# Sixty 128-wide turns moved from TensorE to VectorE's 32x32 blocks, with short-piece transfers that place the blocks

## The chip, the cores and the metric

The kernel runs on one core of one Trainium2 chip. The metric is device time in microseconds (us) of one execution, as a median of runs; lower is better. On the core, TensorE (PE) does matrix products and turns (transposes through an identity matrix) into PSUM banks, VectorE (DVE) and ScalarE (ACT) do element-wise work and empty the banks, GpSimd (POOL) does small work, and SyncE (SP) issues nearly all transfers (DMAs) in one queue, in order.

## What is computed

One layer of an encoder for two groups of tokens: 512 prompt tokens and 64 sample tokens that have caches. All in float32.

```
xn   = rmsnorm(x, ln_mix);  proj = xn @ w_in        # conv input, z, gates, q/k/v of differential attention
h    = x + [gated delta net ; differential attention] @ w_out
mk   = rmsnorm(mem, ln_mem_kv) @ w_mem_k            # prompt: from 256 memory rows; also an output
mv   = rmsnorm(mem, ln_mem_kv) @ w_mem_v            # also an output
h    = h + softmax(q mk^T) mv @ w_mem_o             # sample: mk, mv come from cache_mem_k, cache_mem_v
h    = h + relu(rmsnorm(h) @ w_ff1)^2 @ w_ff2
y    = rmsnorm(h, ln_final)
```

The keys of the differential attention of the sample are `cache_diff_k` (256 rows) and 64 new rows; the new keys of both groups are outputs too (`o_dk_p`, `o_dk_s`). `rmsnorm(x, g)` is x times g times one over the root of the mean square of the row.

## The kernel before

**Layout.** Activations lie turned: feature on the 128 partitions, token along the row. `project` multiplies weight blocks of 128 columns with them. Each float32 weight is split in a high part `wh` (ACT cast, L573) and a remainder `wl` (DVE, L574), and products are done in three terms. A weight block of 512 KB is loaded by SP at L564 or L569 into one of four `raw` buffers.

**Order.** The program is traced in one order and then rearranged: `Arrangement` (L161 to L328) plays it through with a model of each engine's times (`Step.cost`, L119), picks at each step what can start first, and fixes the order of every engine's queue by `arrange` (L419). For a DMA it takes 530 ns of SP's time (L405), a rate by row length (L138) and 2500 ns to spare on the landing (L407). The order of PE's queue is thus fixed when the program is built. Of SP's transfers that are ready, the one traced first goes first.

**Where data must be turned.** Four places have rows where columns are needed, or the reverse, and use `tr` (L532), a PE instruction on a 128x128 block that writes a PSUM bank with tag `ba`:

- *Memory rows*: `mt` (L1040) holds the 256 memory rows of 1024, loaded in one DMA (L1041). `turn_memory` (L1350) takes the squares (ACT, L622), the root (DVE and POOL), multiplies root and gain row `gkv` in (L1352, helper L632), turns 16 blocks (L1354) and splits them into `mh` and `ml` (L1356, L1357). These are the fixed operands of the two memory projections from L1619; these put their banks in `dst` at L1639.
- *Key output*: in `diff_project` (L1406) the key projection of each of four heads arrives turned in `kdT`. `evac` turns 2 blocks per half of the prompt and 1 of the sample (L1461, L1463), copies them to `ko` (L1471, L1474) and stores them (L1472, L1475). `ko` shares the two buffers `p0` with `ckr[0]` and with the softmax tiles of `diff_head` (L1507). Behind it SP places the stacked copies of keys and queries (L1437, L1456, L1458) that the scores read.
- *Cached keys*: `diff_cache` (L1481) loads 256 rows in 2 DMAs (L1485), turns 8 blocks (L1488) and copies them to `ckT` (L1489). The sample's scores read it (L1496).
- *Cached memory keys*: `cm` (L1709) is loaded in one DMA (L1710) into storage slot 5 once the product with `w_out` has read that slot; 16 blocks are turned (L1722) and split into `cmT` and `cml` (`split_turned`, L1596). Slot 5 next takes the first memory attention output `mo` (L1770), written at L1784 and L1785.

Of the kernel before, what the change touches and what calls it, by code (L numbers as in the profile page):

```python
# [9 lines left out]
F32 = mybir.dt.float32  # L10
# [421 lines left out]
def hybrid_layer_kernel(  # L432
# [76 lines left out]
    def small(tag, shape, bufs=None, dt=F32):  # L509
        tag = SHARED.get(tag, tag)  # L510
        bufs = 1 if tag in ("vn", "on", "S", "qz", "an", "B0") or tag[:-1] in ("At", "Dt", "Y") else 2
        return sp.tile(shape, dt, tag=tag, name=nm(tag), bufs=bufs)
# [19 lines left out]
    def tr(out, in_):  # L532
        n = in_.shape[0]
        nc.tensor.transpose(out, in_, ident[:n, :n])  # L534
# [10 lines left out]
    def gain_rows(g, tag):  # L545
        gB = cp.tile([P, D], F32, tag=tag, name=nm("gB"))
        nc.sync.dma_start(gB, g.partition_broadcast(P))
        return gB
# [71 lines left out]
    def squares(dst, src, n):  # L620
        s1 = tiny([P, 1])
        A.activation(dst[:n], src[:n], AF.Square, accum_out=s1[:n])  # L622
        return s1

    def root(s1, n, total=None):
        r1 = tiny([P, 1])
        V.tensor_scalar(s1[:n], s1[:n] if total is None else total, 1.0 / D, EPS, ALU.mult, ALU.add)
        rpow(r1[:n], s1[:n])
        return r1

    def scale(dst, src, r1, gB, n, c=slice(0, D)):
        V.scalar_tensor_tensor(dst[:n, c], src[:n, c], r1[:n], gB[:n, c], ALU.mult, ALU.mult)  # L632
# [234 lines left out]
    with after(last_traced()):  # L867
        G.memset(triu, 1.0)
        G.affine_select(out=triu, in_=triu, pattern=[[1, P]], compare_op=ALU.is_ge, fill=0.0, base=0, channel_multiplier=-1)
    G_Q, G_FF, G_FIN = 16, 24, 32  # L870
    gn = gcol[:, 40:41]
    dn = const([P, 1], "dn")
    V.tensor_scalar(dn, gcol[:, 41:42], 1.0 - LAM0, None, ALU.mult)
# [165 lines left out]

    mt = view(e3, 0, 2, D)  # L1040
    nc.sync.dma_start(mt, mem_prompt[0].rearrange("(b p) d -> p b d", p=P))  # L1041
    gkv = gain_rows(ln_mem_kv[0], "qz1")
    mn = view(e5, 0, 2, D)
    mhl = pair(4, F32R)
    mh, ml = view(mhl, 0, KT, NMEM), view(mhl, 1, KT, NMEM)
# [26 lines left out]
    def v4(ap, nb):  # L1072
        return ap.rearrange("p (h n) -> p h n", h=4)[:, :nb, :]

    def sb(tag, bufs=2):
        return small(tag, [P, 4, P], bufs)

    zs, zsample = (
        ap.rearrange("p (h t) -> p h t", h=H)
# [269 lines left out]

    def turn_memory():  # L1350
        for bi in range(2):
            scale(mn[:, bi, :], mt[:, bi, :], root(squares(mn[:, bi, :], mt[:, bi, :], P), P), gkv, P)  # L1352
            for q in range(2):
                src = turn(mn[:, bi, :], P, q, "ba")  # L1354
                mhi, mlo = (x[:, 4 * q : 4 * q + 4, bi * P : (bi + 1) * P] for x in (mh, ml))
                A.copy(mhi, src)  # L1356
                V.tensor_tensor(mlo, src, mhi.bitcast(F32), ALU.subtract)  # L1357

    S, behind = None, lambda: None
    prepared = [gdn_prep(*chunks[0])]  # L1360
# [39 lines left out]
    with after(*behind_keys):  # L1400
        G.memset(qz[64:, :64], 0.0)
        G.memset(qz[:64, 64:], 0.0)
        G.memset(vs[64:], 0.0)
    stacked = {}

    def diff_project(h):  # L1406
        hs = slice(h * P, (h + 1) * P)
        if h < 2:
            qn = [od[:, 2 * h + j, :SEQ].bitcast(F32R) for j in range(2)]
        else:  # L1410
            qn = [small(tag, [P, SEQ], dt=F32R) for tag in ("Y0", "Y1")]
        tags = ("kd", "vb", "X", "KQ") if h % 2 else ("At0", "At1", "Dt0", "Dt1")
        ks = [small(tag, [P, SEQ], dt=F32R) for tag in tags]
        stacked[h] = ks[:2], ks[2:]
        for kind, base in (("q", 2056), ("k", 2568), ("v", 3080)):
            def evac(b, a0, n):
                first_half = a0 == 0
                t0 = slice(0, 256) if first_half else slice(256, SEQ)

                def parts(dst, src):  # L1420
                    A.copy(dst[0][:, t0], src)
                    V.tensor_tensor(dst[1][:, t0], src, dst[0][:, t0].bitcast(F32), ALU.subtract)

                if kind == "q":
                    d = qn[1][:, t0].bitcast(F32)
                    with tc.high_priority():
                        scaled(d, b[:, :256], a0)
                        parts(qn, d)
                    if first_half:
                        for c in range(2):  # L1430
                            R = slice(64 * c, 64 * c + 64)
                            V.tensor_tensor(qz[R, R], b[R, 256:], rB[R, 256:320], ALU.mult)
                    else:
                        for c in range(2):
                            R = slice(64 * c, 64 * c + 64)
                            for j in range(2):
                                nc.sync.dma_start(  # L1437
                                    qs[h % 2][64 * j : 64 * j + 64, c, :SEQ].bitcast(F32), qn[j][R].bitcast(F32)
                                )
                    return  # L1440
                if kind == "v":
                    d = small("zr", [P, 320])
                    dp_, ds = d[:, :256], d[:, 256:]
                else:
                    dp_, ds = kdT[:, h, t0], kdT[:, h, SEQ:T]
                with tc.high_priority():
                    scaled(dp_, b[:, :256], a0)
                    if first_half:
                        scaled(ds, b[:, 256:], 256)
                if kind == "k":  # L1450
                    parts(stacked[h][0], dp_)
                    if not first_half:
                        first_, second_ = ([x.bitcast(F32) for x in pair_] for pair_ in stacked[h])
                        for j in range(2):
                            for R in (slice(0, 64), slice(64, P)):
                                nc.sync.dma_start(second_[j][R], first_[j][64:])  # L1456
                        for j in range(2):
                            nc.sync.dma_start(first_[j][64:], first_[j][:64])  # L1458
                bt = bank()
                for t in range(2):  # L1460
                    tr(bt[:, t * P : (t + 1) * P], dp_[:, t * P : (t + 1) * P])  # L1461
                if first_half:
                    tr(bt[:DEC, 256:384], ds)  # L1463
                src, t2 = bt[:, :256].rearrange("p (t d) -> p t d", t=2), slice(t0.start // P, t0.start // P + 2)
                if kind == "v":
                    A.copy(vtm[:, t2, hs], src)
                    if first_half:
                        A.copy(vs[:DEC, h, :], bt[:DEC, 256:384])
                else:
                    ko = small("ko", [P, 3, P])  # L1470
                    A.copy(ko[:, :2], src)  # L1471
                    nc.sync.dma_start(o_dk_p[0, 0, t0, h, :].rearrange("(t p) d -> p t d", p=P), ko[:, :2])  # L1472
                    if first_half:
                        A.copy(ko[:DEC, 2], bt[:DEC, 256:384])  # L1474
                        nc.sync.dma_start(o_dk_s[0, 0, :, h, :], ko[:DEC, 2])  # L1475

            project(weights(w2, base + h * P), xs, evac, halves=GATHERED)
        nc.sync.dma_start(o_dv_p[0, 0, :, h, :].rearrange("(t p) d -> p t d", p=P), vtm[:, :, hs])
        nc.sync.dma_start(o_dv_s[0, 0, :, h, :], vs[:DEC, h, :])

    def diff_cache():  # L1481
        ckr = [small("p0", [P, 512]), small("p1", [P, 512])]
        nc.sync.dma_start(cvv, cache_diff_v[0, 0].rearrange("(b p) h d -> p b (h d)", p=P))
        for bi in range(2):
            nc.sync.dma_start(ckr[bi], cache_diff_k[0, 0, bi * P : (bi + 1) * P].rearrange("p h d -> p (h d)"))  # L1485
            b = bank()
            for h in range(H):
                tr(b[:, h * P : (h + 1) * P], ckr[bi][:, h * P : (h + 1) * P])  # L1488
            A.copy(ckT[:, :, bi * P : (bi + 1) * P], v4(b, 4))  # L1489

    def sample_rows(h, hs, so, on):

# [126 lines left out]
    for w, out in ((w_mem_k, o_mk), (w_mem_v, o_mv)):  # L1619
        dst = tokens  # L1620
        for f in range(2):
# [14 lines left out]
                                start=(k == 0 and j == 0), stop=(k == KT - 1 and j == 2),  # L1636
                            )
            for t in range(2):
                (A.copy if t else V.tensor_copy)(dst[:, t, fs], bs[t])  # L1639
                if out is o_mv:  # L1640
                    A.copy(mv[:, t, fs], dst[:, t, fs])
                    V.tensor_tensor(mvl[2 * t + f], dst[:, t, fs], mv[:, t, fs].bitcast(F32), ALU.subtract)
# [63 lines left out]
    V.tensor_scalar(shrink16, cols, -1.0 / 16, None, ALU.mult)  # L1706


    cm = view(pair(5), 0, 2, D)  # L1709
    nc.sync.dma_start(cm, cache_mem_k[0, 0].rearrange("(b p) h d -> p b (h d)", p=P))  # L1710
    cmu = pair(2, F32R)
    cmv = [small(tag, [P, 512]) for tag in ("X", "X", "B0", "B0")]
    for j, cv_ in enumerate(cmv):
# [2 lines left out]
    cmT, cml = (view(cmu, i, KT, NMEM) for i in range(2))  # L1716
    mkl, cml = ([x.rearrange("p (j n) -> p j n", j=2) for x in mkl], [cml[:, 2 * i : 2 * i + 2, :] for i in range(4)])
    for k2 in range(KT // 2):
        b = bank()
        for kk in range(2):  # L1720
            for bi in range(2):
                tr(b[:, kk * 256 + bi * P : kk * 256 + (bi + 1) * P], cm[:, bi, (2 * k2 + kk) * P : (2 * k2 + kk + 1) * P])  # L1722
        split_turned(cmT[:, 2 * k2 : 2 * k2 + 2, :], cml[k2], b)

    mo = []
    for h in range(H):
# [557 lines left out]
```

## Time and profile before

| | |
|---|---|
| median of 3 runs | 919.6 us (919.39 to 919.87) |
| the profiled execution, its own time | 918.87 us |
| its span | 917.1 us |
| PE busy | 907.4 us |
| DVE busy | 763.0 us |
| ACT busy | 622.3 us |
| turns of the four places, on PE | 16 + 20 + 8 + 16 = 60 |

The span runs from the first to the last instruction of the profile; 1.8 us of the execution lie around it. "Busy" of PE is a union of instruction spans whose ends are modelled, so a few tenths of a us between starts can be waits. Turns carry the line of the helper, L534, and name the bank (`ba`, `g`) and the tile (`u` for the large tiles, `p` for `p0` and `p1`). A merged row of the timeline gives the start of its first instruction, the time to the end of its last, and the count.

### The profile page before, as it was taken

How to read it: one execution, taken by the hardware profiler on the slowest of the kernel's cores; microseconds unless marked ns; L12 is line 12 of the kernel's file. 1: busy time of each engine (PE TensorE's matmuls, PEld its weight loads, DVE VectorE, ACT ScalarE, POOL GpSimd, SP SyncE). 2: the span in 40 equal slices, each digit the busy share in tenths (PEclk: the TensorE clock that was granted, in tenths of full speed). 3: DMA queues.
4: the chain of work that ended last, by engine and by line, in shares of the span. 5: the costliest groups of instructions: out<-in, count | busy, mean ns of one | idle time of the engine just before them, and what ended most of it. 6: DMA issues, size and time to landing. Idle time of an engine off the chain costs nothing.

```text
span 917.1 us, 17313 instructions
## 1 busy us (share of the span) xinstructions
PE 907.4 (99%) x6482; PEld 873.6 (95%) x6482; DVE 763.0 (83%) x1658; ACT 622.3 (68%) x1418; POOL 71.6 (8%) x165
## 2 busy tenths in 40 slices
PE   8999999999999999999999999999999999999997
PEld 7999999999999888999999999999999999999986
DVE  6878887988787776666557989999999999999995
ACT  6564885535566664435445658878888888888855
POOL 2452112110010000000000000000000000000001
PEclk9999999999999999999999999999999999999999
DMA  6923411116444857341211322332323223322313
GB/s 200 300 64 92 117 54 36 36 47 175 119 120 113 280 191 206 86 129 56 59 46 51 112 68 76 99 94 87 108 92 94 92 93 93 92 93 93 115 48 104
DMA packets 112287, 96.97 MB, mean 106 GB/s; under 512 B 6888, under 2 KB 99274, under 8 KB 111690
## 3 DMA queue, kind: packets, MB, share of 16 engines
q1 hardware_dynamic: 111450, 94.67, 34.7%
q8 instruction: 51, 0.84, 0.4%
q10 hardware_dynamic: 656, 1.18, 0.4%
q14 instruction: 34, 0.28, 0.1%
q0 software_dynamic: 96, 0.00, 0.0%
HBM read 80.85 MB, written 9.75 MB: 99 GB/s over the span
## 4 chain that ended last, share of the span: by engine, by line
PE 95%; ACT 3%; DVE 1%; DMA 1%; issue 0%; SPq 0%; ACTq 0%
PE pr L530 57%; PE g L530 13%; PE ba L530 12%; PE gs L530 7%; PE ba L534 3%; PE g L534 2%; ACT w L1806 1%; DMA raw<-in_w_in_dram 1%; DVE w L1807 0%; ACT wl L1806 0%; ACT pr L2064 0%; PE gs L534 0%; PE ba L2156 0%; PE pr L2156 0%; ACT wh L1806 0%; DVE raw L1902 0%
## 5 line engine op out<-in xcount | busy, mean ns | idle before, releaser
L530 PE MATMUL pr<-u,wh 128*128 128x320 f32 (+3 forms) x1608 | 364.9, 317 | 1.6 <-ACT wh L726 0.9
L530 PEld LDWEIGHTS pr<-u,wh 128*128 128x128 f32 x1608 | 262.1, 189 | 10.9 <-ACT u L793 1.1
L530 PE MATMUL pr<-u,wl 128*128 128x320 f32 (+2 forms) x984 | 256.9, 299 | 0.0
L530 PEld LDWEIGHTS pr<-u,wl 128*128 128x128 f32 x984 | 174.2, 189 | 1.0
L573 ACT CAST wh<-raw 128x1024 fp32r<-128x1024 f32 x65 | 68.3, 1050 | 62.8 <-PE pr L530 52.2
L574 DVE TENSOR_TENSOR wl<-raw,wh 128x1024 fp32r<-128x1024 f32 x65 | 79.4, 1222 | 26.7 <-ACT wh L573 26.1
L1807 DVE TENSOR_TENSOR w<-raw,w 128x512 fp32r<-128x512 f32 x89 | 60.1, 688 | 6.5 <-PE pr L530 2.3
L1806 ACT CAST w<-raw 128x512 fp32r<-128x512 f32 x89 | 52.9, 619 | 3.2 <-DVE raw L1902 2.3
L530 PE MATMUL ba<-u,wl 128*128 128x288 f32 x360 | 52.6, 295 | 0.0
L2067 ACT COPY u<-pr 128x288 f32<-128x288 f32 x116 | 46.1, 398 | 5.6 <-PE pr L530 3.9
L530 PEld LDWEIGHTS ba<-u,wl 128*128 128x128 f32 x360 | 49.3, 188 | 0.0
L530 PE MATMUL pr<-x,w 128*128 128x288 f32 x252 | 46.9, 294 | 0.0
L530 PE MATMUL pr<-u,w 128*128 128x288 f32 x252 | 46.9, 294 | 0.0
L530 PE MATMUL pr<-wh,u 128*128 128x512 f32 x128 | 41.8, 399 | 0.0
L2064 ACT COPY pr<-u 128x288 f32<-128x288 f32 x100 | 39.5, 403 | 2.7 <-DVE u L2069 1.0
L2069 DVE TENSOR_TENSOR u<-u,pr 128x288 f32<-128x288 f32 x80 | 35.9, 450 | 6.2 <-PE pr L530 5.9
L1807 DVE TENSOR_TENSOR wl<-raw,wl 128x512 fp32r<-128x512 f32 x58 | 39.0, 684 | 0.2
L530 PEld LDWEIGHTS pr<-x,w 128*128 128x128 f32 x252 | 38.0, 187 | 0.0
L530 PEld LDWEIGHTS pr<-u,w 128*128 128x128 f32 x252 | 38.0, 188 | 0.0
L1806 ACT CAST wl<-raw 128x512 fp32r<-128x512 f32 x58 | 34.3, 621 | 4.2 <-PE ba L530 2.1
L530 PE MATMUL pr<-x,wl 128*128 128x288 f32 x168 | 31.9, 297 | 0.2
L530 PE MATMUL pr<-x,wh 128*128 128x288 f32 x168 | 31.6, 296 | 0.1
(564 smaller groups left out, 2050.8 us busy)
## 6 DMA issues: line engine op xcount, KB each, us to landing
raw<-in_w_ff_dram SPq DMA_DIRECT2D x36, 512.0 KB
raw<-in_w_ff_dram SPq DMA_DIRECT2D x56, 256.0 KB
raw<-in_w_in_dram SPq DMA_DIRECT2D x27, 512.0 KB
raw<-in_w_mem_k_dram SPq DMA_DIRECT2D x8, 512.0 KB
raw<-in_w_mem_v_dram SPq DMA_DIRECT2D x8, 512.0 KB
raw<-in_w_out_dram SPq DMA_DIRECT2D x8, 512.0 KB
raw<-in_w_mem_q_dram SPq DMA_DIRECT2D x8, 512.0 KB
raw<-in_w_mem_o_dram SPq DMA_DIRECT2D x8, 512.0 KB
```

Source lines behind the costliest of these rows:

```text
L530: nc.tensor.matmul(out, lhsT, rhs, start=start, stop=stop, skip_group_check=skip_group_check)
L534: nc.tensor.transpose(out, in_, ident[:n, :n])
L573: A.copy(wh, raw)
L574: V.tensor_tensor(wl, raw, wh.bitcast(F32), ALU.subtract)
L1806: A.copy(hi, src)
L1807: V.tensor_tensor(lo, src, hi.bitcast(F32), ALU.subtract)
L2064: A.copy(b[:, :n], to)
L2067: A.copy(to, b[:, :n])
L2069: V.tensor_tensor(to, to, b[:, :n], ALU.add)
```

## The change

All four places take another way. A 32x32 block is turned inside VectorE (`V.transpose`, one instruction over a whole row of blocks), and a DMA puts the blocks where they belong, for each group of 32 columns one DMA whose contiguous pieces are 32 floats (128 bytes).

- `turned_in`: four DMAs load 256 rows by 128 columns so that the 32x32 blocks lie in the place of their turned position; one `V.transpose` of 128x256 then finishes the turn. Used for the memory rows (8 times, 32 DMAs), the cached keys (4 times, 16 DMAs) and the cached memory keys (8 times, 32 DMAs).
- `turned_out`: `V.transpose` first, then four DMAs store. Used for the key output: per head 8 DMAs for the prompt and 4 for the sample, 48 in all.
- The memory rows are turned unscaled. The gain is multiplied in when they are split (`gcol`, a scalar for each partition), and the root of the norm (`mroot`, a scalar for each row) when the banks of the memory projections are evacuated. The load of the gain rows `gkv` and the two products of L1352 go; the load of `mt` and the squares stay, and the squares write to `mn`, where the new blocks are loaded.

```diff
+    def turned_in(dst, src):
+        for a in range(0, P, 32):
+            rows_ = src[:, a : a + 32].rearrange("(b p) c -> p b c", p=32)
+            nc.sync.dma_start(dst[a : a + 32].rearrange("p (b c) -> p b c", c=32), rows_)
...
-            scale(mn[:, bi, :], mt[:, bi, :], root(squares(mn[:, bi, :], mt[:, bi, :], P), P), gkv, P)
-            for q in range(2):
-                src = turn(mn[:, bi, :], P, q, "ba")
-                mhi, mlo = (x[:, 4 * q : 4 * q + 4, bi * P : (bi + 1) * P] for x in (mh, ml))
-                A.copy(mhi, src)
-                V.tensor_tensor(mlo, src, mhi.bitcast(F32), ALU.subtract)
+            V.tensor_copy(mroot[:, bi : bi + 1], root(squares(mn[:, bi, :], mt[:, bi, :], P), P))
+        apart = view(e5, 0, KT, NMEM)
+        turned = view(e3, 0, KT, NMEM)
+        for k in range(KT):
+            turned_in(apart[:, k], mem_prompt[0, :, k * P : (k + 1) * P])
+        for k in range(KT):
+            V.transpose(turned[:, k], apart[:, k])
+            g = gcol[:, G_KV + k : G_KV + k + 1]
+            A.activation(mh[:, k], turned[:, k], AF.Identity, scale=g)
+            V.scalar_tensor_tensor(ml[:, k], turned[:, k], g, mh[:, k].bitcast(F32), ALU.mult, ALU.subtract)
...
+    def turned_out(dst, src):
+        for a in range(0, P, 32):
+            to = dst[:, a : a + 32].rearrange("(b p) c -> p b c", p=32)
+            nc.sync.dma_start(to, src[a : a + 32].rearrange("p (b c) -> p b c", c=32))
...
-                    ko = small("ko", [P, 3, P])
-                    A.copy(ko[:, :2], src)
-                    nc.sync.dma_start(o_dk_p[0, 0, t0, h, :].rearrange("(t p) d -> p t d", p=P), ko[:, :2])
-                    if first_half:
-                        A.copy(ko[:DEC, 2], bt[:DEC, 256:384])
-                        nc.sync.dma_start(o_dk_s[0, 0, :, h, :], ko[:DEC, 2])
+                ko = small("ko", [P, 3 * P])
+                V.transpose(ko[:, :256], dp_)
+                turned_out(o_dk_p[0, 0, t0, h, :], ko[:, :256])
+                if first_half:
+                    V.transpose(ko[:, 256:320], ds)
+                    turned_out(o_dk_s[0, 0, :, h, :], ko[:, 256:320])
...
-            nc.sync.dma_start(ckr[bi], cache_diff_k[0, 0, bi * P : (bi + 1) * P].rearrange("p h d -> p (h d)"))
-            b = bank()
-            for h in range(H):
-                tr(b[:, h * P : (h + 1) * P], ckr[bi][:, h * P : (h + 1) * P])
-            A.copy(ckT[:, :, bi * P : (bi + 1) * P], v4(b, 4))
+            for i in range(2):
+                h = 2 * bi + i
+                turned_in(ckr[bi][:, i * PAST : (i + 1) * PAST], cache_diff_k[0, 0, :, h])
+            V.transpose(ckT[:, 2 * bi : 2 * bi + 2, :].rearrange("p h n -> p (h n)"), ckr[bi])
...
-                (A.copy if t else V.tensor_copy)(dst[:, t, fs], bs[t])
+                if t:
+                    A.activation(dst[:, t, fs], bs[t], AF.Identity, scale=mroot[:, t : t + 1])
+                else:
+                    V.tensor_scalar(dst[:, t, fs], bs[t], mroot[:, t : t + 1], None, ALU.mult)
...
-    cm = view(pair(5), 0, 2, D)
-    nc.sync.dma_start(cm, cache_mem_k[0, 0].rearrange("(b p) h d -> p b (h d)", p=P))
+    cmp_ = pair(5)
+    cm, ct = (view(cmp_, i, KT, NMEM) for i in range(2))
+    for k in range(KT):
+        turned_in(cm[:, k], cache_mem_k[0, 0, :, k // 2, k % 2 * P : k % 2 * P + P])
...
-        b = bank()
-        for kk in range(2):
-            for bi in range(2):
-                tr(b[:, kk * 256 + bi * P : kk * 256 + (bi + 1) * P], cm[:, bi, (2 * k2 + kk) * P : (2 * k2 + kk + 1) * P])
-        split_turned(cmT[:, 2 * k2 : 2 * k2 + 2, :], cml[k2], b)
+        ks = slice(2 * k2, 2 * k2 + 2)
+        b = ct[:, ks].rearrange("p k n -> p (k n)")
+        V.transpose(b, cm[:, ks].rearrange("p k n -> p (k n)"))
+        split_turned(cmT[:, ks, :], cml[k2], b)
```

More of the change, by code (lines that the diff above doesn't have):

```diff
@@ L869, in hybrid_layer_kernel @@
         G.affine_select(out=triu, in_=triu, pattern=[[1, P]], compare_op=ALU.is_ge, fill=0.0, base=0, channel_multiplier=-1)
-    G_Q, G_FF, G_FIN = 16, 24, 32
+    G_KV, G_Q, G_FF, G_FIN = 8, 16, 24, 32
     gn = gcol[:, 40:41]
@@ L1041, in hybrid_layer_kernel @@
     nc.sync.dma_start(mt, mem_prompt[0].rearrange("(b p) d -> p b d", p=P))
-    gkv = gain_rows(ln_mem_kv[0], "qz1")
+    mroot = const([P, 2], "mroot")
     mn = view(e5, 0, 2, D)
@@ L1458, in evac @@
                             nc.sync.dma_start(first_[j][64:], first_[j][:64])
-                bt = bank()
-                for t in range(2):
-                    tr(bt[:, t * P : (t + 1) * P], dp_[:, t * P : (t + 1) * P])
-                if first_half:
-                    tr(bt[:DEC, 256:384], ds)
-                src, t2 = bt[:, :256].rearrange("p (t d) -> p t d", t=2), slice(t0.start // P, t0.start // P + 2)
-                if kind == "v":
-                    A.copy(vtm[:, t2, hs], src)
+                if kind == "v":
+                    bt = bank()
+                    for t in range(2):
+                        tr(bt[:, t * P : (t + 1) * P], dp_[:, t * P : (t + 1) * P])
+                    if first_half:
+                        tr(bt[:DEC, 256:384], ds)
+                    t2 = slice(t0.start // P, t0.start // P + 2)
+                    A.copy(vtm[:, t2, hs], bt[:, :256].rearrange("p (t d) -> p t d", t=2))
                     if first_half:
                         A.copy(vs[:DEC, h, :], bt[:DEC, 256:384])
-                else:
-                    ko = small("ko", [P, 3, P])
-                    A.copy(ko[:, :2], src)
-                    nc.sync.dma_start(o_dk_p[0, 0, t0, h, :].rearrange("(t p) d -> p t d", p=P), ko[:, :2])
-                    if first_half:
-                        A.copy(ko[:DEC, 2], bt[:DEC, 256:384])
-                        nc.sync.dma_start(o_dk_s[0, 0, :, h, :], ko[:DEC, 2])
+                    return
+                ko = small("ko", [P, 3 * P])
+                V.transpose(ko[:, :256], dp_)
+                turned_out(o_dk_p[0, 0, t0, h, :], ko[:, :256])
+                if first_half:
+                    V.transpose(ko[:, 256:320], ds)
+                    turned_out(o_dk_s[0, 0, :, h, :], ko[:, 256:320])
             project(weights(w2, base + h * P), xs, evac, halves=GATHERED)
```

## The prediction

> **What bounds the kernel.** I read the page's busy lines and chain first, then busy time by stretch.
>
> ```profile
> PE 907.4 (99%) x6482; PEld 873.6 (95%) x6482; DVE 763.0 (83%) x1658; ACT 622.3 (68%) x1418; POOL 71.6 (8%) x165
> PE 95%; ACT 3%; DVE 1%; DMA 1%; issue 0%; SPq 0%; ACTq 0%
> ```
>
> The busy columns of the next rows are PE, PEld, DVE, ACT, POOL; then come the granted clock, the DMA engines' share and GB/s.
>
> ```profile
> 0.00:30.00 30.00, 26.52 (x176) 24.43 (x177) 21.03 (x57) 18.40 (x39) 5.90 (x24) 1.00 0.74 226
> 30.00:100.00 70.00, 70.00 (x533) 70.00 (x532) 57.24 (x119) 41.41 (x63) 29.38 (x71) 1.00 0.46 130
> 100.00:180.00 80.00, 80.00 (x661) 78.94 (x661) 70.40 (x175) 56.38 (x114) 13.74 (x27) 1.00 0.19 52
> 180.00:260.00 80.00, 79.96 (x625) 77.89 (x624) 64.78 (x191) 41.04 (x124) 8.75 (x23) 1.00 0.46 121
> 260.00:360.00 100.00, 100.00 (x621) 89.69 (x621) 75.00 (x187) 64.42 (x168) 4.84 (x10) 1.00 0.60 187
> 360.00:430.00 70.00, 70.00 (x459) 66.21 (x458) 47.19 (x104) 32.38 (x69) 1.17 (x1) 1.00 0.34 101
> 430.00:900.00 470.00, 469.65 (x3366) 457.47 (x3365) 417.33 (x809) 359.95 (x826) 3.94 (x5) 1.00 0.27 83
> 900.00:917.00 17.00, 11.24 (x55) 8.94 (x53) 10.01 (x26) 8.31 (x19) 3.90 (x5) 0.98 0.41 140
> ```
>
> PE stands idle only in the first 30 us and the last 17 us. From 30 to 430 us, where all four turning places lie, it is never seen idle, and the chain is PE for 95% of the span. So an instruction taken off PE there is worth its time on PE, as long as nothing that PE needs comes late. VectorE is second and has 20% free in that stretch (314.6 of 400 us busy).
>
> **What leaves PE.** I measure a turn by the starts around a group, since modelled ends overlap. These rows show memory rows, key output and cached memory keys.
>
> ```profile
> 102.02 0.60 PE L534 MATMUL ba<-ident,u 128*128 128x128 f32 x4
> 102.37 0.49 PE L530 MATMUL pr<-u,wh 128*128 128x256 f32 x2
> 102.70 0.28 PE L530 MATMUL pr<-u,wl 128*128 128x256 f32 x1
> ...
> 104.33 0.40 PE L530 MATMUL pr<-u,wh 128*128 128x256 f32 x2
> 104.57 0.28 PE L530 MATMUL pr<-u,wl 128*128 128x256 f32 x1
> ...
> 208.63 0.49 PE L534 MATMUL ba<-ident,u 128*128 128x128 f32 x3
> 208.88 0.39 PE L530 MATMUL pr<-u,wl 128*128 128x320 f32 x1
> 209.11 0.46 PE L530 MATMUL pr<-u,wh 128*128 128x320 f32 x2
> 209.41 0.27 PE L534 MATMUL g<-ident,Y 128*128 128x128 f32 x1
> ...
> 210.03 0.38 PE L534 MATMUL ba<-ident,u 128*128 128x128 f32 x2
> 210.17 0.39 PE L530 MATMUL pr<-u,wh 128*128 128x320 f32 x1
> 210.40 0.45 PE L530 MATMUL pr<-u,wl 128*128 128x320 f32 x2
> ...
> 414.73 1.03 PE L534 MATMUL ba<-ident,u 128*128 128x128 f32 x8
> 415.52 0.36 PE L530 MATMUL pr<-u,wl 128*128 128x256 f32 x1
> 415.72 0.40 PE L530 MATMUL pr<-u,wh 128*128 128x512 f32 x1
> ```
>
> An undisturbed product step takes 0.12 us on 256 columns (0.24 for two from 104.33) and 0.15 on 320 (0.30 for two from 209.11). Four memory turns: 102.02 to 102.70, less two steps of 0.12, is 0.44. Three key turns: 208.63 to 209.11 less 0.15 is 0.33; two: 210.03 to 210.40 less 0.15 is 0.22. Eight cached ones: 414.73 to 415.72 less 0.12 is 0.87. That is 0.11 us for each turn, in groups of any size. Sixty times 0.11 is **6.6 us**; with what the group boundaries add (102.02 itself starts 0.08 late), I take **6.7**. The lower end is the 0.79 us in which eight started, 0.099 each, 5.9 us. The upper end, from the 0.60 us that four occupy with their overlap, is 0.15 each, 9 us.
>
> **What VectorE and ScalarE get.** Nothing in the trace is a VectorE turn. The nearest rows in shape are these.
>
> ```profile
> L1215 DVE TENSOR_TENSOR Dt<-Dt,g 128x256 f32<-128x256 f32 x20 | 8.4, 420 | 0.7
> L1599 DVE TENSOR_TENSOR u<-ba,u x4: 681/688/692, 416.2 to 419.4; 128x512 fp32r<-128x512 f32 x4
> L1357 DVE TENSOR_TENSOR u<-ba,u x4: 681/682/684, 105.0 to 137.5; 128x512 fp32r<-128x512 f32 x4
> L632 DVE SCALAR_TENSOR_TENSOR u<-u,tiny,gB x2: 1282/1283/1284, 53.0 to 58.7; 128x1024 f32<-128x1024 f32 x2
> L1471 ACT COPY p<-ba 128x256 f32<-128x256 f32 x8 | 3.0, 374 | 1.1 <-PE ba L534 1.0
> ```
>
> I take 0.42 for 128x256 and 0.69 for 128x512; half and double are the ends. Added: 8 memory turns (3.4), 8 remainders with the gain (3.4), 8 key turns (3.4) and 4 small ones (0.8), 2 and 4 turns of 128x512 (4.1): 15 us. Removed: 2 of L632 (2.6) and 4 of L1357 (2.7). VectorE gains about 10 us, against 85 free ones between 30 and 430. At double price for the turns it gains 22, still under the free time. ScalarE loses the eight copies of L1471 and four small ones and cached copies, and gains eight 128x256 splits, so it gets no fuller. The root at L1639 adds a scalar to eight evacuations that run anyway: nothing, hidden by the third `pr` bank; if it isn't hidden, under 0.1 us each.
>
> **What SP and the DMA engines get.** 128 short-piece DMAs (32, 48, 16, 32) come for 16 that go (gain rows 1, stores 12, loads 2 and 1): 112 more. The nearest rows are two of four consecutive 32 KB loads and a stretch of 512-byte weight pieces.
>
> ```profile
> 43.28 0.58 SPq L1382 DMA_DIRECT2D zr<-in_lambda_q_dram  x1
> ...
> 44.86 0.54 SPq L1382 DMA_DIRECT2D zr<-in_lambda_k_dram  x1
> ...
> 51.00:52.00 1.00, 1.00 (x11) 1.00 (x10) 0.96 (x2) 0.00 (x0) 0.88 (x2) 1.00 1.05 309
> ```
>
> Issue period: 43.28 to 44.86 is three, 0.53 us each; 112 make 59 us of SP. A 512-byte piece takes 16 x 512 / 309 GB/s = 26.5 ns on one of 16 engines. A new DMA has 256 pieces, 16 to an engine, so 0.42 us at that piece time, and 0.11 if only bytes counted. SP's issue paces it. I take 0.53; the ends are 0.35 (the shortest issue, below) and 0.85 (pieces at twice the time).
>
> The Trainium skill (DMA: Bandwidth & Descriptors, Specifications) speaks against this change: below 512 bytes a transfer loses line rate, because the engine reads, modifies and writes. The row above has only 512-byte pieces and can't decide it; by that rule a DMA would take about 0.85 us, the third rival below.
>
> **Where lateness could reach PE, place by place.**
>
> ```profile
> L569 SPq DMA_DIRECT2D raw<-in_w_mem_k_dram x8: 373/382/744, 253.2 to 312.9; - x8
> 214.51 0.35 SPq L1485 DMA_DIRECT2D p<-in_cache_diff_k_dram  x1
> 221.12 1.03 PE L534 MATMUL ba<-ident,p 128*128 128x128 f32 x8
> 223.00 0.76 PE L530 MATMUL g<-u,qz 128*128 128x256 f32 x4
> 407.10 0.37 SPq L1710 DMA_DIRECT2D u<-in_cache_mem_k_dram  x1
> L1784 ACT CAST u<-g x8: 217/408/589, 432.8 to 496.5; 128x512 fp32r<-128x512 f32 x4, 128x64 fp32r<-128x64 f32 x4
> line<-rB POOLq DMA_DIRECT2D x1, 2.2 KB, 3.0
> ```
>
> *Memory rows*: before, they were turned at 102 us though scaled by 60; now 32 DMAs (17 us) can start when the squares free `mn`, and the result is needed first by the memory projections, whose weights are issued from 253.2 us. Weights queue behind them on SP, under cover of four `raw` buffers. Cost nothing; without cover, 17 us of SP.
>
> *Key output*: nobody on PE waits for the stores. The new wait is VectorE's for a `p0` buffer, held for 8 x 0.53 + 3.0 = 7.2 us by a store; behind it on VectorE stand the evacuations of the next projection, so PE's `pr` banks. The 36 added DMAs, 19 us, also stand before the stacked copies that the scores need. What covers them is PE's other work in that stretch, the projections of the next head and from 253.2 us those of the memory. I take nothing; uncovered, the nine per head (4.8 us) four times.
>
> *Cached keys*: a buffer's eight DMAs from 214.5 take 4.2, the landing 3.0, the turn 0.7: 222.4, and the scores of 223.00 just make it.
>
> *Cached memory keys*: this is the tight one. All 32 DMAs from 407.1 take 17.0, the landing 3.0, the last turn and the split 2.0: 429.1. The first pair is ready by 416.3, before its scores. But slot 5 goes to `mo`, first written at 432.8, and not before the last block is split. That leaves 3.7 us. A late block would stop ACT at L1784, behind it the banks `g0`, `gs`, `g1`, and PE, whose order is fixed. I take nothing.
>
> **Sum.** 918.87 (the profiled execution, 1.8 of it outside the span) - 6.7 = 912.2. The median lies 0.7 above that execution, so **912.9 us**.
>
> **Rivals.**
>
> 1. *More is gained.* Turns cost up to 0.15 each: 9 us, **910.6**. For it speaks their overlapping span, against it the starts, which say 0.11.
> 2. *VectorE gives half of it back.* Its 10 us fall into a stretch where it is 88% busy (100 to 180) or feeds PE directly. If a third delays what PE waits for, 3.3 are lost: **916.2**. Against it: no wait of PE on VectorE is seen there now.
> 3. *The cached memory keys arrive late.* If a piece takes twice 26.5 ns, a DMA takes 0.85; 32 take 27.2, the last split is at 439.3, 6.5 after 432.8, and the gain is gone: **919.4**. For it: the order is fixed and modelled with a 530 ns issue. Against it: in the run of 512-byte pieces the engines were full at 26.5 ns each, and pieces a quarter as long have less to move. It is what the Trainium skill's rule would do here (DMA: Bandwidth & Descriptors, Specifications).
> 4. *Slower.* The same slot 5, with blocks above 0.91 us each: then the last split is more than 8.5 us late (32 x 0.91 = 29.1), more than the 6.7 gained and 1.8 beside. At twice the issue period, 1.06, it is 13.2 late: **926.1**. For it: neither rate nor issue of such DMAs is in the trace, and shared queues can delay weights too. Against it: SP's issues above take 0.35 to 0.58.
>
> **How the numbers follow.** Forecast 0.60; rival 1, 0.08; rival 2, 0.13; rival 3, 0.10; rival 4, 0.09. A measurement of this kernel tells about 0.2% (1.8 us) from no change. Faster holds the forecast and rivals 1 and 2, 0.81; same is rival 3, 0.10; slower is rival 4, 0.09. The range is 910.3 to 917.7: it takes in the bounds of the turn's cost and rival 2, and leaves out 3 and 4, 0.19.
>
> **What would show it.** Right: 60 fewer L534 rows, PE still without idle from 30 to 430, busy PE lower by about 6 to 7, the memory projections and w_out starting 3 to 5 us earlier, all of it before 430. VectorE turns of 128x256 near 0.42 and DMA issues near 0.53 show the two unknown prices. Wrong: PE waits that name `mo`, ACT L1784, `p0` or a DMA between 200 and 440; short-piece DMAs over 0.9 us apart; or a stretch after 430 that changes its length, which nothing here touches.

## The result, and the profile after

The changed kernel takes **914.24 us** in the median of 4 runs (913.80 to 915.30), the kernel before 919.55 beside it (919.39 to 919.87). The ratio is 0.9941, with a 95% interval of 0.9929 to 0.9954: 5.3 us less, between 4.2 and 6.5. The forecast was 912.9 us with 910.3 to 917.7; the sign and the range were right, and the gain came out 1.4 us smaller than the 6.7 of the sum.

Of the profiled execution of the changed kernel (913.8 us, span 912.1), first the page: the busy line, the share of the chain by engine, and the packets.

```profile
PE 902.7 (99%) x6422; PEld 868.4 (95%) x6422; DVE 771.9 (85%) x1688; ACT 617.1 (68%) x1406; POOL 70.0 (8%) x165
DMA packets 140831, 97.50 MB, mean 107 GB/s; under 512 B 38376, under 2 KB 128458, under 8 KB 140234
PE 94%; ACT 3%; DVE 2%; DMA 0%; issue 0%; POOL 0%; SPq 0%; ACTq 0%; DVEq 0%
```

Sixty instructions have left PE (6482 to 6422). PE's busy time fell by 4.7 us (907.4 to 902.7), VectorE's rose by 8.9 (763.0 to 771.9). PE still makes up nearly the whole chain.

Busy time by stretch, with the columns PE, PEld, DVE, ACT, POOL, granted clock, DMA share, GB/s. The second row is part of the first.

```profile
30.00:430.00 400.00, 399.60 (x2863) 380.81 (x2862) 325.47 (x806) 231.69 (x527) 56.67 (x132) 1.00 0.47 124
...
260.00:360.00 100.00, 99.69 (x608) 87.99 (x607) 81.54 (x205) 64.98 (x170) 8.10 (x15) 1.00 0.64 189
```

PE is idle for 0.40 of the 400 us; before, the five rows from 30 to 430 added up to 0.04. Most of it, 0.31, lies between 260 and 360, where VectorE went from 75.0 to 81.5 busy.

**A finer ruler.** The first work on a weight starts between 28.2 and 30.4 us in the profiles of this study, before any of the four places, so spans carry 2 us of scatter that has nothing to do with the change. The latest, 30.4, is in an execution of 919.81 us of a kernel whose median is 918.34 (e3 below). A cast of a weight block on ACT (L573) occurs 65 times in every kernel, up to 532 us. The start of the 64th less the start of the first is a stretch that holds all four places and little else. The rows are the first, the 46th (in the product with `w_out`) and the 64th, from the timeline of ACT; first the kernel before, then the changed one.

```profile
28.19 1.06 ACT L573 CAST wh<-raw 128x1024 fp32r<-128x1024 f32 x1 [3.44 <-PE pr L530]
...
375.37 1.06 ACT L573 CAST wh<-raw 128x1024 fp32r<-128x1024 f32 x1 [1.79 <-PE pr L530]
...
525.75 1.05 ACT L573 CAST wh<-raw 128x1024 fp32r<-128x1024 f32 x1
```

```profile
28.63 1.05 ACT L573 CAST wh<-raw 128x1024 fp32r<-128x1024 f32 x1 [3.43 <-PE pr L530]
...
372.09 1.05 ACT L573 CAST wh<-raw 128x1024 fp32r<-128x1024 f32 x1 [1.79 <-PE pr L530]
...
520.97 1.05 ACT L573 CAST wh<-raw 128x1024 fp32r<-128x1024 f32 x1
```

Before: 525.75 - 28.19 = 497.56. After: 520.97 - 28.63 = 492.34, so **5.22 us less**. Up to the 46th cast it is 347.18 against 343.46, 3.72 less; the cached memory keys, which lie behind it, bring the other 1.50. From the 64th cast to the end of the span nothing changed: 391.35 (917.1 - 525.75) and 391.13. The rerun of the changed kernel (below) gives 492.32 (28.68 to 521.00), so this ruler repeats to a few hundredths.

**The new operations.** VectorE's turns by line and form; in each row the count, then the total in us and the mean in ns.

```profile
L1485 DVE STREAM_TRANSPOSE p<-u 128x256 f32<-128x256 f32 x8 | 3.4, 420 | 0.0
L1363 DVE STREAM_TRANSPOSE u<-u 128x256 f32<-128x256 f32 x8 | 3.3, 428 | 0.0
L1739 DVE STREAM_TRANSPOSE u<-u 128x512 f32<-128x512 f32 x4 | 2.8, 703 | 0.0
L1502 DVE STREAM_TRANSPOSE u<-p 128x512 f32<-128x512 f32 x2 | 1.4, 707 | 0.0
L1488 DVE STREAM_TRANSPOSE p<-u 128x64 f32<-128x64 f32 x4 | 0.8, 206 | 0.0
```

The turns cost 0.42 and 0.70 us, where 0.42 and 0.69 were taken.

The loads of the cached memory keys, from SP's timeline, and the DMA view of the 17 us from 404 to 421 in which they run (its first lines: packets, and the share of queue q1).

```profile
403.82 16.91 SPq L1081 DMA_DIRECT2D u<-in_cache_mem_k_dram  x32
```

```profile
DMA packets 8247, 1.03 MB, mean 60 GB/s; under 512 B 8244, under 2 KB 8244, under 8 KB 8244
## 3 DMA queue, kind: packets, MB, share of 16 engines
q1 hardware_dynamic: 8244, 1.00, 38.1%
```

32 issues take 16.91 us, 0.53 each; the prediction had 17.0 for the 32. In these 17 us nearly every packet is one of the 128-byte pieces: 0.381 x 16 engines x 17 us / 8244 is **12.6 ns a piece**, half of the 26.5 of a 512-byte piece. So a DMA of 256 pieces keeps each engine busy for 0.20 us and SP for 0.53: SP's issue sets the pace and the engines stand more than half empty.

### The profile page after: what moved, and what is told of

It reads as the page before. It is cut to its first block, busy times and chain, and to the rows that moved or that the text cites. A ratio compares the mean times of both kernels' runs of the same rounds, so it can differ in the third digit from the quotient of the medians.

```text
span 912.1 us, 17358 instructions
## 1 busy us (share of the span) xinstructions
PE 902.7 (99%) x6422; PEld 868.4 (95%) x6422; DVE 771.9 (85%) x1688; ACT 617.1 (68%) x1406; POOL 70.0 (8%) x165
## 4 chain that ended last, share of the span: by engine, by line
PE 94%; ACT 3%; DVE 2%; DMA 0%; issue 0%; POOL 0%; SPq 0%; ACTq 0%; DVEq 0%
PE pr L530 57%; PE g L530 13%; PE ba L530 12%; PE gs L530 7%; PE ba L534 2%; PE g L534 2%; ACT w L1823 1%; DMA u<-in_x_prompt_dram 0%; ACT wl L1823 0%; DVE w L1824 0%; ACT pr L2081 0%; PE gs L534 0%; PE pr L2173 0%; PE ba L2173 0%; ACT wh L1823 0%
## 5 line engine op out<-in xcount | busy, mean ns | idle before, releaser
L573 ACT CAST wh<-raw 128x1024 fp32r<-128x1024 f32 x65 | 68.2, 1049 | 60.9 <-PE pr L530 53.3
```

The costliest lines, as they stand in the source:

```text
L573: A.copy(wh, raw)
```

## The experiments

The theories after the result: either a turn is worth 0.11 us on PE, as the prediction measured it, and about 1.3 us of the 6.6 was lost elsewhere; or a turn is worth only 0.09 and 5.3 is all there was. And if something is lost, is it at one of the four places?

### Each place alone

Four kernels, each the kernel before with one place changed. The edits are the parts of the diff above that belong to the place:

```diff
# e1: 16 turns
+            turned_in(apart[:, k], mem_prompt[0, :, k * P : (k + 1) * P])
+            V.transpose(turned[:, k], apart[:, k])
...
+                    A.activation(dst[:, t, fs], bs[t], AF.Identity, scale=mroot[:, t : t + 1])
# e2: 20 turns
+                V.transpose(ko[:, :256], dp_)
+                turned_out(o_dk_p[0, 0, t0, h, :], ko[:, :256])
...
# e3: 8 turns
+                turned_in(ckr[bi][:, i * PAST : (i + 1) * PAST], cache_diff_k[0, 0, :, h])
+            V.transpose(ckT[:, 2 * bi : 2 * bi + 2, :].rearrange("p h n -> p (h n)"), ckr[bi])
# e4: 16 turns
+        turned_in(cm[:, k], cache_mem_k[0, 0, :, k // 2, k % 2 * P : k % 2 * P + P])
...
+        V.transpose(b, cm[:, ks].rearrange("p k n -> p (k n)"))
```

> Only the memory rows take the new way (16 turns off PE, 32 short-piece loads, the root at the evacuation). Theory A, each turn is worth its PE time and nothing is lost: 16 x 0.11 = 1.8 us faster than before. Theory B, the 1.4 us missing in the whole change were lost at one place: 1.8 here, unless this is the place, then about 0.4. Theory C, a turn is worth less than 0.11 everywhere, 5.3 / 60 = 0.088: 1.4 us faster.

> Only the key output takes the new way (20 turns off PE, 48 short-piece stores, VectorE waits for a p0 buffer). Theory A: 20 x 0.11 = 2.2 us faster than before. Theory B, with the loss here, because the stores hold p0 and stand on SP before the stacked copies: 0.8 us faster. Theory C: 1.8 us faster.

> Only the cached keys take the new way (8 turns off PE, 16 short-piece loads). Theory A: 8 x 0.11 = 0.9 us faster than before. Theory B, with the loss here, because the keys land just when the scores need them: 0.5 us slower. Theory C: 0.7 us faster.

> Only the cached memory keys take the new way (16 turns off PE, 32 short-piece loads). Theory A: 16 x 0.11 = 1.8 us faster than before. Theory B, with the loss here, because slot 5 is given late to the attention output: 0.4 us faster. Theory C: 1.4 us faster.

| changed alone | median (kernel before 919.29) | ratio, 95% | stretch from first to 64th cast | less than before |
|---|---|---|---|---|
| memory rows (e1) | 917.77 | 0.9981 (0.9972 to 0.9990) | 495.99 | 1.57 |
| key output (e2) | 917.04 | 0.9979 (0.9970 to 0.9988) | 495.40 | 2.16 |
| cached keys (e3) | 918.34 | 0.9991 (0.9982 to 1.0000) | 496.63 | 0.93 |
| cached memory keys (e4) | 917.65 | 0.9981 (0.9972 to 0.9990) | 495.98 | 1.58 |

The stretches come from these rows of ACT's timeline, in the order of the table; the first three show the 46th cast too.

```profile
29.27 1.05 ACT L573 CAST wh<-raw 128x1024 fp32r<-128x1024 f32 x1 [3.42 <-PE pr L530]
...
374.68 1.05 ACT L573 CAST wh<-raw 128x1024 fp32r<-128x1024 f32 x1 [1.79 <-PE pr L530]
...
525.26 1.05 ACT L573 CAST wh<-raw 128x1024 fp32r<-128x1024 f32 x1
```

```profile
28.71 1.05 ACT L573 CAST wh<-raw 128x1024 fp32r<-128x1024 f32 x1 [3.45 <-PE pr L530]
...
373.77 1.05 ACT L573 CAST wh<-raw 128x1024 fp32r<-128x1024 f32 x1 [1.79 <-PE pr L530]
...
524.11 1.05 ACT L573 CAST wh<-raw 128x1024 fp32r<-128x1024 f32 x1
```

```profile
30.36 1.05 ACT L573 CAST wh<-raw 128x1024 fp32r<-128x1024 f32 x1 [3.44 <-PE pr L530]
...
376.61 1.05 ACT L573 CAST wh<-raw 128x1024 fp32r<-128x1024 f32 x1 [1.79 <-PE pr L530]
...
526.99 1.05 ACT L573 CAST wh<-raw 128x1024 fp32r<-128x1024 f32 x1
```

```profile
29.23 1.05 ACT L573 CAST wh<-raw 128x1024 fp32r<-128x1024 f32 x1 [3.44 <-PE pr L530]
...
525.21 1.05 ACT L573 CAST wh<-raw 128x1024 fp32r<-128x1024 f32 x1
```

Theory B is out: no place gives away 1.4 us by itself; each brings about what its turns cost (0.10 to 0.12 us a turn). Between A and C these four do not decide: e2 and e3 meet A (2.2 and 0.9), e1 and e4 lie halfway to C. Together the four bring 1.57 + 2.16 + 0.93 + 1.58 = **6.24**, the whole change 5.22. The last place is additive: 1.58 alone, 1.50 within the change. The missing 1.0 arises before the 46th cast: there the first three alone are 1.77, 2.12 and 0.93 shorter, together 4.82, and the whole change 3.72. The first three without the fourth were not run.

### The price of a turn

The kernel before with each of the 60 turns made twice, and then five times, into the same place of the same bank; TensorE gets 60 and 240 turns more, and nothing else changes.

```diff
-            if by is None:
-                tr(o, f)
+            if by is None:
+                for _ in range(5):
+                    tr(o, f)
...
```

> The kernel before with each of the 60 turns of the four places done twice on PE into the same bank. Theory A, a turn in its place costs PE 0.11: 6.6 us slower than before. Theory C, 0.088: 5.3 us slower. If PE were not the bound at these places, less than 3 us.

> The kernel before, with each of the 60 turns made five times, 240 turns more on TensorE and nothing else. Theory T (a turn in these places costs 0.11 us, as the starts in the trace say, so that the change took 6.6 off TensorE and about 1.3 was lost elsewhere): 26.4 us more, ratio 1.029. Theory U (a turn costs 0.09 us, so that the 5.3 measured is all that the 60 turns were worth and nothing was lost): 21.6 us more, ratio 1.0235.

Twice: 925.39 against 919.96 us, ratio 1.0065 (1.0052 to 1.0078), which is 4.8 to 7.2 us and holds both. Five times: **945.94** against 920.04, ratio 1.0284 (1.0270 to 1.0298). That holds 1.029 and excludes 1.0235. The rows of twice, then of five times:

```profile
30.02 1.05 ACT L573 CAST wh<-raw 128x1024 fp32r<-128x1024 f32 x1 [3.44 <-PE pr L530]
...
533.90 1.05 ACT L573 CAST wh<-raw 128x1024 fp32r<-128x1024 f32 x1
```

```profile
28.55 1.05 ACT L573 CAST wh<-raw 128x1024 fp32r<-128x1024 f32 x1 [3.44 <-PE pr L530]
...
552.30 1.05 ACT L573 CAST wh<-raw 128x1024 fp32r<-128x1024 f32 x1
```

Twice, the stretch is 503.88, 6.32 longer: 0.105 us a turn. Five times, it is 523.75, 26.19 longer: **0.109 us a turn**. So the sixty were worth 6.3 to 6.5 on PE, and the theory of the cheaper turn falls.

### The additions without the gain

The changed kernel, with 60 turns of a constant put back on TensorE in the old groups; nobody reads them.

```diff
+    def idle_turns(n):
+        b = bank()
+        for i in range(n):
+            tr(b[:, i * P : (i + 1) * P], ident)
...
+            idle_turns(4)
             V.transpose(ckT[:, 2 * bi : 2 * bi + 2, :].rearrange("p h n -> p (h n)"), ckr[bi])
...
```

> The changed kernel with 60 turns of a constant put back on TensorE at the four places, in the old groups, whose results nobody reads: all that the change adds, without what it takes away. Theory T (about 1.3 us is lost on VectorE, ScalarE or the queues): 1 to 1.5 us above the kernel before, 920.5 to 921. Theory U (nothing is lost): the kernel before within 0.4 us, ratio 0.9995 to 1.0005.

> The changed kernel itself, for a closer time beside the same runs of the kernel before. The four parts alone gave 0.8 to 2.3 us each, 6.3 together; the whole change gave 5.3. If the parts add up: 6.3 us less, ratio 0.9931. If something is lost when they stand together, or the sum is only scatter: 5.3 less, ratio 0.9942.

With idle turns: 919.41 against 920.04, ratio 0.9997 (0.9988 to 1.0006). The changed kernel again, beside it: 914.30, ratio 0.9939 (0.9927 to 0.9952), 5.6 less. The rows of the kernel with idle turns:

```profile
30.21 1.05 ACT L573 CAST wh<-raw 128x1024 fp32r<-128x1024 f32 x1 [3.42 <-PE pr L530]
...
527.92 1.05 ACT L573 CAST wh<-raw 128x1024 fp32r<-128x1024 f32 x1
```

Its stretch is 497.71, only 0.15 longer than before. So the transfers, the work of VectorE and SP's 112 issues cost nearly nothing **while PE has the 60 turns to do**. Neither theory had this: the price of the turn is T's, and the cost of the additions U's. One reading that fits both, and is not shown, is a cover that thins out: with the turns gone, PE comes sooner to work that others have not finished. The idle turns wait for no data, though, so they are a better cover than the old ones were. Another reading is the order of the work, below.

### Places in pairs

Three kernels with two of the first three places changed, to see which two lose the 1.0. The edits are those of e1 to e3, two at a time.

> Memory rows and key output together (36 turns), cached keys of both kinds as before. Measured by the trace, from the first weight cast near 28 us to that near 526 us, the parts alone shorten this stretch by 1.57 and 2.14. Theory L (these two load VectorE and together they lose what the whole change loses): about 2.7 less. Theory P (the loss of 1.0 needs all three places ahead of 350 us, or falls differently in each order of the work): 3.4 to 3.9 less.

> Key output and cached keys together (28 turns). The parts alone shorten the same stretch by 2.14 and 0.93. Theory L' (both lie between 210 and 260 us, share SP and the p0 buffers, and lose there): about 2.1 less. Theory P: 2.8 to 3.3 less.

> Memory rows and cached keys together (24 turns). The parts alone shorten the same stretch by 1.57 and 0.93. Theory L'' (these two lose together): about 1.5 less. Theory P: 2.2 to 2.7 less.

One execution each. The rows, in this order:

```profile
29.13 1.05 ACT L573 CAST wh<-raw 128x1024 fp32r<-128x1024 f32 x1 [3.43 <-PE pr L530]
...
522.93 1.05 ACT L573 CAST wh<-raw 128x1024 fp32r<-128x1024 f32 x1
```

```profile
30.01 1.05 ACT L573 CAST wh<-raw 128x1024 fp32r<-128x1024 f32 x1 [3.44 <-PE pr L530]
...
524.57 1.05 ACT L573 CAST wh<-raw 128x1024 fp32r<-128x1024 f32 x1
```

```profile
29.76 1.05 ACT L573 CAST wh<-raw 128x1024 fp32r<-128x1024 f32 x1 [4.46 <-PE pr L530]
...
524.75 1.05 ACT L573 CAST wh<-raw 128x1024 fp32r<-128x1024 f32 x1 [0.53 <-PE pr L530]
```

| pair | less than before | sum of its parts |
|---|---|---|
| memory rows and key output (e10) | 3.76 | 3.73 |
| key output and cached keys (e11) | 3.00 | 3.09 |
| memory rows and cached keys (e12) | 2.57 | 2.50 |

Every pair adds up to within 0.1, so no pair is to blame, and L, L' and L'' are out. What is left is theory P, and it has two halves: the loss needs all three places, or it falls differently in each order of the work.

Where it shows: between 30 and 430 us the profile names one wait of the changed kernel's PE. In the timelines of PE and VectorE it stands at the end of the differential attention:

```profile
337.48 0.62 PE L530 MATMUL pr<-wh,u 128*128 128x512 f32 x2
338.34 0.66 PE L534 MATMUL ba<-ident,an 128*128 128x128 f32 x4 [0.24 <-DVE Dt L1612]
...
339.07 0.62 PE L530 MATMUL pr<-wh,u 128*128 128x512 f32 x2
339.53 0.40 PE L530 MATMUL pr<-wl,u 128*128 128x512 f32 x1
```

```profile
336.86 0.83 DVE L1585 TENSOR_TENSOR an<-an,ta 128x640 f32<-128x640 f32 x1 [0.74 <-POOL ta L618]
337.60 0.69 DVE L1612 TENSOR_TENSOR Dt<-ba,u 128x512 fp32r<-128x512 f32 x1
```

VectorE waits 0.74 us for the norm's power on POOL, scales `an`, then takes a remainder out of a `ba` bank until 338.29; PE's turn of `an` needs a `ba` bank and starts at 338.34. Two products of 512 columns take 0.46 between starts where nothing disturbs them (339.07 to 339.53), so from 337.48 PE was due at 337.94: 0.40 are lost here. The kernel before does the same turn without a wait; so does the pair e10, and in the kernel with idle turns the wait is gone. The other 0.6 shows as no idle time of PE that the profile names.

A wait that can be seen is not yet a loss against the sum of the parts, though. In e12, which adds up, PE waits longer, for a stacked copy that SP issued behind the cached keys' loads:

```profile
241.95 0.44 PE L530 MATMUL g<-At,qs 128*128 128x128 f32 x2 [0.83 <-DMA At<-At]
```

And the order of PE's work is not the same either, since the build arranges every version anew. Two marks from PE's timelines are the first turn of `an` (first head) and the first product of the memory projections; first the kernel before, then the changed one.

```profile
261.41 0.60 PE L534 MATMUL ba<-ident,an 128*128 128x128 f32 x4
...
302.00 0.48 PE L530 MATMUL pr<-wh,u 128*128 128x512 f32 x1
```

```profile
267.35 0.60 PE L534 MATMUL ba<-ident,an 128*128 128x128 f32 x4
...
291.54 0.63 PE L530 MATMUL pr<-wh,u 128*128 128x512 f32 x2
```

In the changed kernel the head's turn comes 5.9 us later and the projections start 10.5 us earlier. So the 1.0 can be a cover that is too thin, or an order that happens to pack worse in this version. No run holds the order fixed, so the cause stays open.

### Lateness of the cached memory keys

The changed kernel with each of the 32 loads of the tightest place cut in two, 64 issues for the same pieces and bytes.

```diff
-        turned_in(cm[:, k], cache_mem_k[0, 0, :, k // 2, k % 2 * P : k % 2 * P + P])
+        for r in range(2):
+            turned_in(cm[:, k, r * P : (r + 1) * P], cache_mem_k[0, 0, r * P : (r + 1) * P, k // 2, k % 2 * P : k % 2 * P + P])
```

> The changed kernel with each load of the cached memory keys cut in two (64 of 16 KB for 32 of 32 KB), so that at 0.53 us per issue the last lands 17 us later. Theory S, slot 5 hands the lateness on to the attention output and PE, whose order is fixed: PE stands idle between 425 and 445 us and the time is 3 to 13 us longer than the changed kernel's, 917 to 927. Theory F, the order written for this kernel puts query projections of later heads there and nothing shows: 914 to 915. If the pieces and not the issue set the pace, the 64 loads take no longer than the 32: 914 to 915, with the last issue near 421.

914.94 against 919.96 us, ratio 0.9950 (0.9935 to 0.9965): 4.6 us less than the kernel before. That is the time of theory F. From SP's timeline, and from ACT's the first writing of `mo` (in the storage tile `u`), with the same of the changed kernel last:

```profile
404.13 32.69 SPq L1081 DMA_DIRECT2D u<-in_cache_mem_k_dram  x64
```

```profile
28.98 1.05 ACT L573 CAST wh<-raw 128x1024 fp32r<-128x1024 f32 x1 [3.44 <-PE pr L530]
...
444.51 0.58 ACT L1802 CAST u<-g 128x512 fp32r<-128x512 f32 x1
...
522.11 1.05 ACT L573 CAST wh<-raw 128x1024 fp32r<-128x1024 f32 x1
```

```profile
431.37 0.59 ACT L1801 CAST u<-g 128x512 fp32r<-128x512 f32 x1 [0.80 <-DVE u L1612]
```

The 64 issues end at 436.8, 16.1 us later than the 32 did (420.7), at 0.51 each: the issue sets the pace, not the pieces. The work on `mo` began at 444.51 instead of 431.37, 13.1 later. Yet the stretch is only 0.79 longer (493.13 against 492.34). The arrangement knew of the 64 issues, and PE does query projections (`pr`) up to 446.7, where the changed kernel goes on to scores at 438.2; so the blocks' lateness was nearly free. About half of the 0.79 did not come by way of `mo`: PE's one named wait behind 430 us is for the remainder of the sixth query weight, whose load stood behind the 64 on SP (issued at 436.93, in the changed kernel at 420.83).

```profile
445.92 0.39 PE L530 MATMUL pr<-u,wl 128*128 128x256 f32 x1 [0.41 <-DVE wl L574]
```

What a delay costs that the arrangement does not know of was not tried.

No version that was run beats the changed kernel.

## Why the prediction was right, and where it was too high

**What bounds the kernel.** Right in the main. PE stays the chain (94%), and of the 6.3 to 6.5 us of turns taken off it 5.2 come back as time; the stretch behind the 64th cast keeps its length.

**The price of a turn.** Right in its unit: 0.11 from the starts, 0.105 measured over 60 added turns and 0.109 over 240. The bounds 0.099 and 0.15 were not needed. The forecast added 0.1 for group boundaries (6.7); 6.3 to 6.5 is what the sixty are worth.

**The term that was mis-sized** is the 6.7 of the sum, taken to come back whole. The ruler gives 5.22; 1.1 to 1.3 us did not come back. A little of it is missing in the parts already, which make 6.24; about 1.0 is lost only in the whole change. Its cause is not shown. The part that can be seen, 0.4, is a wait of the kind that rival 2 named, PE on VectorE; rival 2 put it at 3.3 us and gave it 0.13. That VectorE's fuller load brings it is not shown either: with the idle turns VectorE is nearly as busy between 260 and 360 (80.9 against 81.5), and no wait of PE is named there. "No wait of PE on VectorE is seen there now" was true of the order before, and said nothing of how close such a wait was or of the order that the changed program would get.

**The new prices.** VectorE's turns and SP's issue came out as taken (0.42, 0.70 and 0.53). VectorE gained 8.9 in all instead of 10, and ScalarE got no fuller (622.3 to 617.1), as forecast.

**Pieces of 128 bytes.** Rivals 3 and 4 needed a DMA of 0.85 us and more; it is 0.53 of issue, and 0.20 of engine time at 12.6 ns a piece. The Trainium skill (DMA: Bandwidth & Descriptors, Specifications) says that transfers below 512 bytes miss line rate. The trace agrees in direction: 128 bytes in 12.6 ns are 10 GB/s on an engine, 512 in 26.5 are 19. A piece at double time was the prediction's own reading of the rule, and the trace disagrees with it: half the rate at a quarter of the bytes is half the time. Behind an issue of 0.53 the lower rate does not show in the time.

**The four places.** Right for the changed kernel, that nobody waits: no PE wait names `mo`, `p0`, ACT's writing of `mo` or a DMA. The reasons were half wrong, for "PE, whose order is fixed" holds only after the build. For the cached memory keys the numbers fit (issues 16.91 for 17.0), but the arrangement prices the new DMAs and puts other work ahead, so the 3.7 us of slack at `mo` was not the true limit; with 64 issues it was overrun at a cost of 0.8, half of that through a weight queued behind them. For the cached keys, loads from 214.5 that "just make it" were not put to the test: the changed kernel issues the last eight from 176.90 to 180.7. A late stacked copy, feared under key output, does show in another version: in e12 PE waits 0.83 us for one.

**The signs named.** Sixty fewer rows: yes. The product with `w_out` 3 to 5 us earlier: yes, 3.28 on the clock and 3.72 by the ruler. The memory projections 3 to 5 us earlier: no, 10.5, because their place in the order changed. PE without idle: nearly, 0.40 of 400. PE busy lower by 6 to 7: no, 4.7; the shortfall shows there too.

## What to carry to other kernels

When an engine is the chain for 95% of the span, its start-to-start time is a good first price for work taken off it; here 5.2 of about 6.4 us came back. Savings that add up one by one and in pairs need not add up all together, so measure them together too. Where the build arranges the work anew, two versions differ in their order as well, and a difference of 1 us between them has no single cause until the order is held fixed. Before a rule on small transfers is feared, divide the time per DMA into issue and engine time: here the issue (0.53 us) hid the pieces (0.20). To compare two profiles closer than their spans allow, take the starts of one instruction that both have, before and behind the changed region.

## What had not been expected of the hardware

- A 128-byte piece keeps a DMA engine busy for 12.6 ns, less than half of a 512-byte one (26.5).
- VectorE turns 32x32 blocks of float32 in the time of an elementwise operation of the same size: 0.42 us for 128x256 against 0.42 for the difference of a tile and a bank (L1215), 0.70 for 128x512 against 0.68 for such a difference (L1357).
- Up to the first weight cast, executions of nearly the same program differ by 2 us (28.2 to 30.4), as much as the largest of the four parts is worth; behind it two profiles of the same kernel agree to 0.02.
